# Gate and up products of a decoder's feed-forward as seven block products in place of eight

## The chip, the cores and the metric

The kernel runs on one core of one Trainium2 chip. The metric is the time of one execution on the device in microseconds (us); less is better. Five engines work from queues of their own and wait for each other by semaphores: TensorE (PE in the profile; its weight loads are PEld), VectorE (DVE), ScalarE (ACT), GpSimd (POOL) and SyncE (SP), which issues the DMAs.

## The reference, cut to what matters

Two layers, each with three groups of attention heads and then a feed-forward. Here only the feed-forward matters: 512 tokens, 1024 features, 2816 hidden features.

```python
for l in range(DEPTH):                      # DEPTH = 2
    x = x + concat(o_fox, o_diff, o_dsa) @ w_out[l]
    h = rms_norm(x, ffn_norm[l])
    gate, up = split(h @ w_gate_up[l], 2)   # 1024 x 2816 each
    x = x + (silu(gate) * up) @ w_down[l]
```

## The kernel before, in words

Everything is held transposed, features on the 128 partitions and the 512 tokens along a row; x is eight tiles of 128x512. Products are made at nearly float32 precision in three passes: each operand is split into a high part (ACT copies it to the rounded type fp32r) and a low part (what is left, a subtraction of two SBUF tiles, mostly on DVE), and `mm3` adds high x high, low x high and high x low into one PSUM tile (L172 to L174 of the profile).

The feed-forward of a layer (`feed_forward`):

- `split_input` makes yh and yl, the high and low parts of x times the norm's gain, eight tiles of each. `square_sum` adds the squares of x into `acc` (DVE, L213). `token_rms` sums `acc` over partitions on PE (ssq, L220) and takes the reciprocal root (the chain ends in r, L187). `norm_row` spreads r over partitions with four transposes on PE (rrow, L991) and copies it to R (L992). R is multiplied in after the products, so the products don't wait for it.
- The 2816 hidden features are 22 tiles of 128. For each tile f, `gate_up(f)` loads 2 x 512 KB of weights (u = 0 gate, u = 1 up; SP, L153), splits them (`weights`: ACT L159, DVE L162, four pieces of 128x512 each) and makes two products, each 8 x 3 matmuls of 128x512. `activate(f)` multiplies by R out of PSUM (DVE L964, L967), takes silu (ACT L965), multiplies gate and up (L968), and splits the result for the down product (gh by ACT L970, gl by DVE L972).
- `down` multiplies three groups of hidden tiles by w_down and adds to x (L984). The first group stands after tile 8, the second half after tile 15 and half after tile 21, the third at the end.

What sets the order: PE's queue is in program order (`manual_schedule`). The queues of ACT, DVE, POOL and SP come from the tile framework's scheduler, which takes priorities from the table AHEAD. Tile pools with a fixed number of buffers set what waits for what: a tile can be written again when its last reader is done. In the attention stages POOL makes low parts too (L162, `wl_in`, and L347, L550); in the feed-forward it has no work.

In the code `G` is POOL, `V` is DVE, `A` is ACT, `T` is PE and `SY` is SP.

Of the kernel before, what the change touches and what calls it, by code (L numbers as in the profile page):

```python
# [11 lines left out]
F32 = mybir.dt.float32  # L12
F32R = mybir.dt.float32r
# [4 lines left out]
P = 128  # L18
# [68 lines left out]
def trunk(ctx: ExitStack, tc: tile.TileContext, x_in, w_in, w_out, w_gu, w_dn, vecs, gfeat, rope, out):  # L87
# [9 lines left out]
    def mm_tile(name):  # L97
        return psum.tile([P, S], F32, tag="mm", name=name, bufs=3)
# [4 lines left out]
    def o_tile(name):  # L103
# [123 lines left out]
    def attention(l, ap):  # L227


        lam_init = 0.8 - 0.6 * math.exp(-0.3 * l)  # L230

        def xt_tile(name):
            return ap.tile([P, S], F32, tag="x", name=name, bufs=5)


        vec = const.tile([P, NV], F32, tag="vec", name=f"vec{l}")
        fb = vec[:, 0:FOX]
        fqn, fkn = vec[:, 8:72], vec[:, 72:136]
        dqn, dkn = vec[:, 136:168], vec[:, 168:200]
# [691 lines left out]
            pass  # L931

    def feed_forward(l, fp):
        y = split_input(l, 1, range(KT))
        acc = square_sum(fp, f"1{l}")
        R = fp.tile([P, S], F32, tag="R", name=f"R{l}")

        def gate_up(f, between=None):

            pgu = []  # L940
            for u in range(2):
                if u and between:
                    between()
                part = weights(w_gu[l, :, (2 * f + u) * KT * P:(2 * f + u + 1) * KT * P], KT * P, P, f"gu{l}_{f}_{u}")
# [17 lines left out]
        def activate(f, pgu):
            gs = fp.tile([P, S], F32, tag="gs", name=f"gs{l}_{f}", bufs=2)
            V.tensor_tensor(gs, pgu[0], R, op=ALU.mult)  # L964
            A.activation(gs, gs, AF.Silu)  # L965
            us = fp.tile([P, S], F32, tag="us", name=f"us{l}_{f}", bufs=2)
            V.tensor_tensor(us, pgu[1], R, op=ALU.mult)  # L967
            V.tensor_tensor(us, us, gs, op=ALU.mult)  # L968
            h = fp.tile([P, S], F32R, tag="gh", name=f"gh{l}_{f}", bufs=16)
# [28 lines left out]
        for f, ps in enumerate((pgu, nxt, after)):  # L998
            activate(f, ps)
        for f in range(3, NF):  # L1000
            activate(f, gate_up(f))

            if f == DOWN_GROUPS[0][1]:
                down(0, range(KT))
            if f == DOWN_GROUPS[1][1]:
                down(1, range(KT // 2))
        down(1, range(KT // 2, KT))
        down(2, range(KT))
# [75 lines left out]
```

## Time and profile before

| | |
|---|---|
| median of 3 runs | 1297.68 us (1296.26 to 1298.03) |
| the profiled execution, its own time | 1296.69 us |
| its span, first to last instruction | 1295.0 us |
| PE busy | 1270.0 us (98%) |
| DVE busy | 802.4 us (62%) |
| ACT busy | 653.9 us (50%) |
| POOL busy | 246.7 us (19%) |
| mean granted TensorE clock | 0.997 |

A span is the time between the first and the last instruction; the time of an execution is some 1.7 us longer. Busy shares are means over stages with different limits, and PE's is no measure of how close it is to its peak, since matmuls are pipelined: the spacing of their starts is what counts.

### The profile page before, as it was taken

Reading aid. Unit: us, or ns where it says so; the run is one execution under the profiler, and the core shown is the slowest. Engines: PE = TensorE matmul, PEld = TensorE weight load, DVE = VectorE, ACT = ScalarE, POOL = GpSimd, SP = SyncE. Lnnn points to the kernel's source line nnn. Section 1 sums busy time; section 2 is a strip of 40 time slices with the busy share of each in tenths; the row PEclk is TensorE's granted clock in tenths of the full one; section 3 lists DMA queues with packets and bytes.
Section 4 is the critical chain, followed back from the end, with each engine's and each line's share of the span. In section 5 each row is a group of like instructions: output and inputs, shape, how many; then the busy total and the mean of one; then the engine's idle time right before and its main releaser. Section 6 shows DMA issues by size and latency. Waiting matters only on the chain. (4 is left out here: it accounts for less than half of the span.)

```text
span 1295.0 us, 19339 instructions
## 1 busy us (share of the span) xinstructions
PE 1270.0 (98%) x7070; PEld 1081.2 (83%) x7070; DVE 802.4 (62%) x1829; ACT 653.9 (50%) x1510; POOL 246.7 (19%) x269
## 2 busy tenths in 40 slices
PE   9999999999999999999999899999999999999998
PEld 8988796788888888888899888968888888888887
DVE  5699996875544455444546999768755534444442
ACT  6678777864332233232456786768543323333321
POOL 2454465220000000000025545552100000000000
PEclk9999999999999999999999999999999999999999
DMA  5321121123333333332322212211333333333332
GB/s 183 90 76 51 56 86 34 57 70 102 105 94 93 96 96 93 110 94 87 103 79 82 75 50 63 66 45 52 96 98 98 97 92 92 97 100 102 92 95 99
DMA packets 34623, 111.55 MB, mean 86 GB/s; under 512 B 3952, under 2 KB 4448, under 8 KB 34528
## 3 DMA queue, kind: packets, MB, share of 16 engines
q1 hardware_dynamic: 34528, 110.31, 28.8%
q8 instruction: 56, 0.92, 0.3%
q14 instruction: 39, 0.32, 0.1%
HBM read 108.14 MB, written 2.15 MB: 85 GB/s over the span
## 5 line engine op out<-in xcount | busy, mean ns | idle before, releaser
L172 PE MATMUL gu<-yh,wh_gu 128*128 128x512 f32 x688 | 268.1, 390 | 0.0
L174 PE MATMUL gu<-yl,wh_gu 128*128 128x512 f32 x688 | 267.7, 389 | 0.0
L173 PE MATMUL gu<-yh,wl_gu 128*128 128x512 f32 x688 | 267.7, 389 | 0.0
L159 ACT ACTIVATE wh_gu<-raw_gu 128x512 fp32r<-128x512 f32 x176 | 111.0, 631 | 254.9 <-PE gu L174 205.6
L172 PE MATMUL pj<-wh_in,yh 128*128 128x256 f32 (+1 forms) x704 | 202.2, 287 | 0.9 <-ACT wh_in L159 0.7
L162 DVE TENSOR_TENSOR wl_gu<-raw_gu,wh_gu 128x512 fp32r<-128x512 f32 x176 | 121.8, 692 | 125.6 <-ACT wh_gu L159 123.1
L173 PE MATMUL pj<-wh_in,yl 128*128 128x256 f32 (+1 forms) x704 | 199.0, 283 | 0.4 <-DVE yl L201 0.4
L174 PE MATMUL pj<-wl_in,yh 128*128 128x256 f32 (+1 forms) x704 | 198.9, 283 | 0.2 <-DVE wl_in L162 0.2
L162 POOL TENSOR_TENSOR wl_in<-raw_in,wh_in 128x512 fp32r<-128x512 f32 x72 | 100.1, 1407 | 488.5 <-ACT wh_in L159 482.3
L172 PEld LDWEIGHTS gu<-yh,wh_gu 128*128 128x128 f32 x688 | 129.1, 188 | 26.8
L174 PEld LDWEIGHTS gu<-yl,wh_gu 128*128 128x128 f32 x688 | 129.1, 188 | 26.8
L173 PEld LDWEIGHTS gu<-yh,wl_gu 128*128 128x128 f32 x688 | 129.1, 188 | 26.8
L172 PE MATMUL dn<-gh,wh_dn 128*128 128x512 f32 x352 | 138.7, 394 | 0.0
L174 PE MATMUL dn<-gl,wh_dn 128*128 128x512 f32 x352 | 138.0, 392 | 0.0
L159 ACT ACTIVATE wh_dn<-raw_dn 128x512 fp32r<-128x512 f32 x96 | 57.3, 597 | 159.6 <-PE dn L174 111.5
L172 PEld LDWEIGHTS pj<-wh_in,yh 128*128 128x128 f32 x704 | 134.5, 191 | 3.0 <-issue 1.2
L173 PE MATMUL dn<-gh,wl_dn 128*128 128x512 f32 x352 | 136.6, 388 | 0.0
L173 PEld LDWEIGHTS pj<-wh_in,yl 128*128 128x128 f32 x704 | 134.9, 192 | 1.3 <-DVE yl L201 0.6
L174 PEld LDWEIGHTS pj<-wl_in,yh 128*128 128x128 f32 x704 | 134.8, 192 | 0.4 <-DVE wl_in L162 0.4
L162 DVE TENSOR_TENSOR wl_dn<-raw_dn,wh_dn 128x512 fp32r<-128x512 f32 x96 | 62.2, 648 | 68.7 <-ACT wh_dn L159 67.7
L174 PEld LDWEIGHTS dn<-gl,wh_dn 128*128 128x128 f32 x352 | 66.1, 188 | 15.5
L173 PEld LDWEIGHTS dn<-gh,wl_dn 128*128 128x128 f32 x352 | 66.1, 188 | 14.8
(323 smaller groups left out, 2167.9 us busy)
## 6 DMA issues: line engine op xcount, KB each, us to landing
raw_gu<-in_w_gu SPq DMA_DIRECT2D x88, 512.0 KB
raw_in<-in_w_in SPq DMA_DIRECT2D x39, 512.0 KB
raw_dn<-in_w_dn SPq DMA_DIRECT2D x32, 448.0 KB
raw_dn<-in_w_dn SPq DMA_DIRECT2D x16, 512.0 KB
cr<-rtd_c SPq DMA_DIRECT2D x12, 256.0 KB
raw_o_fox<-in_w_out SPq DMA_DIRECT2D x8, 384.0 KB
x<-in_x_in SPq DMA_DIRECT2D x8, 256.0 KB
raw_o_diff<-in_w_out SPq DMA_DIRECT2D x4, 512.0 KB
```

What stands on the lines that cost most here:

```text
L159: A.activation(h[:, :w], raw[:, o:o + w], AF.Copy)
L162: eng.tensor_tensor(lo[:, :w], raw[:, o:o + w], f32(h[:, :w]), op=ALU.subtract)
L172: T.matmul(ps, ah, bh, start=first, stop=False, skip_group_check=True)
L173: T.matmul(ps, al, bh, start=False, stop=False, skip_group_check=True)
L174: T.matmul(ps, ah, bl, start=False, stop=last, skip_group_check=True)
```

## The change

From the fourth tile on (`DIRECT = 3`) the gate and up products of a tile are made by `seven(f)` in place of `gate_up` and `activate`. The weights of a tile are a matrix of two row blocks (gate, up) by two column blocks (features 0 to 511 and 512 to 1023): a11, a12, a21, a22, each 128x512 in SBUF. The input is cut into four blocks too: two halves of the features by two halves of the tokens. Seven products of one weight block (or sum of blocks) with one input block (or sum) give all four blocks of the result, in Winograd's form of Strassen's scheme. Each product is 4 x 3 matmuls of 128x256.

- The four input sums of each of the four pairs of feature tiles are made once per layer by POOL (`input_sums`, 16 operations of 128x256) and split by ACT and DVE (8 operations each).
- The four weight sums of each tile are made by POOL (128x512 each), and the seven weight operands are split by ACT and DVE: seven operations of 128x512 each where there were four.
- After each product DVE (once ACT) combines halves: six DVE operations of 128x256 with one operand in PSUM, one of 128x256 in SBUF, and POOL multiplies the up half by R (128x512).
- `norm_row` stands ahead of the third tile, not in the middle of it.
- The hidden tiles of the down product are grouped (0, 7), (7, 14), (14, 22), each group's product in one piece; the tiles gh and gl have 8 buffers in place of 16, and some constants moved into the attention's pool, so that all fits in SBUF.

```diff
-DOWN_GROUPS = [(0, 8), (8, 15), (15, 22)]
+DOWN_GROUPS = [(0, 7), (7, 14), (14, 22)]
...
+        def input_sums(kt):
+            xg = []
+            for m in (kt, kt + KT // 2):
+                t = fp.tile([P, S], F32, tag="ws", name=f"xg{l}_{m}", bufs=5)
+                A.activation(t, x[m], AF.Copy, scale=gf[:, (2 * l + 1) * KT + m:(2 * l + 1) * KT + m + 1])
+                xg.append(t)
...
+            G.tensor_tensor(t1, b12, b11, op=ALU.subtract)
+            G.tensor_tensor(t3, b22, b12, op=ALU.subtract)
+            G.tensor_tensor(t2, b22, t1, op=ALU.subtract)
+            G.tensor_tensor(t4, b21, t2, op=ALU.subtract)
...
+        def seven(f):
...
+            a11, a12, a21, a22 = (r[:, o:o + half] for r in raws for o in (0, half))
+            sums = [fp.tile([P, half], F32, tag="ws", name=f"ws{l}_{f}_{i}", bufs=5) for i in range(4)]
+            with ahead("fh"):
+                G.tensor_tensor(sums[0], a21, a22, op=ALU.add)
+                G.tensor_tensor(sums[1], sums[0], a11, op=ALU.subtract)
+                G.tensor_tensor(sums[2], a11, a21, op=ALU.subtract)
+                G.tensor_tensor(sums[3], a12, sums[1], op=ALU.subtract)
...
+            def product(ps, w, k, first, last):
+                for kt in range(KT // 2):
+                    cs = slice(kt * P, (kt + 1) * P)
+                    mm3(ps, w[0][:, cs], w[1][:, cs], *Y[kt][k], first and kt == 0, last and kt == KT // 2 - 1)
...
+            product(a, whole(a11, "a"), "11", True, True)
+            with ahead("post"):
+                A.activation(u2, a, AF.Copy)
+            product(b, split_sum(sums[1], f"{l}_{f}_1", V), "T2", True, True)
+            with ahead("post"):
+                V.tensor_tensor(u2, b, u2, op=ALU.add)
+            product(d, split_sum(sums[2], f"{l}_{f}_2", V), "T3", True, True)
+            with ahead("post"):
+                V.tensor_tensor(us[:, H:], d, u2, op=ALU.add)
+            product(c, split_sum(sums[0], f"{l}_{f}_0", V), "T1", True, True)
+            with ahead("post"):
+                V.tensor_tensor(us[:, H:], c, us[:, H:], op=ALU.add)
+            product(a, whole(a12, "b"), "21", False, True)
+            with ahead("post"):
+                V.tensor_tensor(gs[:, :H], a, R[:, :H], op=ALU.mult)
+            product(d, whole(a22, "d"), "T4", False, True)
+            with ahead("post"):
+                V.tensor_tensor(us[:, :H], d, u2, op=ALU.add)
+            G.tensor_tensor(us, us, R, op=ALU.mult)
+            product(c, split_sum(sums[3], f"{l}_{f}_3", V), "22", False, True)
+            with ahead("post"):
+                V.tensor_tensor(gs[:, H:], c, u2, op=ALU.add)
+            V.tensor_tensor(gs[:, H:], gs[:, H:], R[:, H:], op=ALU.mult)
+            A.activation(gs, gs, AF.Silu)
+            V.tensor_tensor(us, us, gs, op=ALU.mult)
+            inner(f, us)
...
-        after = gate_up(2, norm_row)
...
+        for kt in range(KT // 2):
+            input_sums(kt)
+        norm_row()
...
+        for f in range(DIRECT, NF):
+            seven(f)
+
+            for g in range(len(DOWN_GROUPS) - 1):
+                if f == DOWN_GROUPS[g][1]:
+                    down(g, range(KT))
+        down(len(DOWN_GROUPS) - 1, range(KT))
```

(The last lines of `seven` are as in `activate`: `inner` splits us into gh and gl. `whole` and `split_sum` are one ACT copy and one DVE subtraction of 128x512 each.)

DVE's queue while PE makes tile 11 of layer 0 (wl_gu and wsl are low parts of weights, ws the sums that POOL makes). Before, a stretch in which one tile's work stands:

```order
L972 TENSOR_TENSOR gl0_10_5367<-us0_10_5362,gh0_10_5365 128x512
L162 TENSOR_TENSOR wl_gu0_12_0_512_5457<-raw_gu0_12_0_5449,wh_gu0_12_0_512_5455 128x512
L964 TENSOR_TENSOR gs0_11_5439<-gu0_11_0_5379,R0_4178 128x512
L162 TENSOR_TENSOR wl_gu0_12_1_0_5488<-raw_gu0_12_1_5484,wh_gu0_12_1_0_5486 128x512
L162 TENSOR_TENSOR wl_gu0_12_1_512_5492<-raw_gu0_12_1_5484,wh_gu0_12_1_512_5490 128x512
L967 TENSOR_TENSOR us0_11_5442<-gu0_11_1_5414,R0_4178 128x512
L162 TENSOR_TENSOR wl_gu0_13_0_0_5533<-raw_gu0_13_0_5529,wh_gu0_13_0_0_5531 128x512
L968 TENSOR_TENSOR us0_11_5442<-us0_11_5442,gs0_11_5439 128x512
```

And now, twelve of a tile's sixteen rows; the other four are u2 of product b ahead of them, and, behind them, the low part of the weights' sum 1 of tile 13, the product of us and gs, and the low part of a22 of tile 13:

```order
L975 TENSOR_TENSOR gl0_10_5943<-us0_10_5816,gh0_10_5941 128x512
L1023 TENSOR_TENSOR wsl_0_12_2_6146<-ws0_12_2_6097,wsh_0_12_2_6144 128x512
L1067 TENSOR_TENSOR us0_11_5962<-gu0_11_d_5960,u20_11_5963 128x256
L1023 TENSOR_TENSOR wsl_0_12_0_6163<-ws0_12_0_6095,wsh_0_12_0_6161 128x512
L1070 TENSOR_TENSOR us0_11_5962<-gu0_11_c_5958,us0_11_5962 128x256
L1023 TENSOR_TENSOR wsl_0_12_3_6215<-ws0_12_3_6098,wsh_0_12_3_6213 128x512
L1073 TENSOR_TENSOR gs0_11_5961<-gu0_11_a_5957,R0_4178 128x256
L1047 TENSOR_TENSOR wl_gu0_13_a_6258<-raw_gu0_13_0_6237,wh_gu0_13_a_6256 128x512
L1076 TENSOR_TENSOR us0_11_5962<-gu0_11_d_5960,u20_11_5963 128x256
L1047 TENSOR_TENSOR wl_gu0_13_b_6326<-raw_gu0_13_0_6237,wh_gu0_13_b_6324 128x512
L1080 TENSOR_TENSOR gs0_11_5961<-gu0_11_c_5958,u20_11_5963 128x256
L1081 TENSOR_TENSOR gs0_11_5961<-gs0_11_5961,R0_4178 128x256
```

Eight operations a tile became sixteen, and between a combination out of PSUM (gu) and the next there now stands one low part of the next tile's or the next but one's weights.

POOL's queue over the same tile, empty before (ws 0 to 3 are the four sums):

```order
L1077 TENSOR_TENSOR us0_11_5962<-us0_11_5962,R0_4178 128x512
L1037 TENSOR_TENSOR ws0_14_1_6388<-ws0_14_0_6387,raw_gu0_14_0_6383 128x512
L1038 TENSOR_TENSOR ws0_14_2_6389<-raw_gu0_14_0_6383,raw_gu0_14_1_6385 128x512
L1039 TENSOR_TENSOR ws0_14_3_6390<-raw_gu0_14_0_6383,ws0_14_1_6388 128x512
L1036 TENSOR_TENSOR ws0_15_0_6797<-raw_gu0_15_1_6795 128x512
L1077 TENSOR_TENSOR us0_12_6108<-us0_12_6108,R0_4178 128x512
```

Five operations a tile, and the product of us and R, which DVE's product of us and gs waits for, stands behind the sums of tiles further on.

PE's queue where the transposes for R stand in layer 0. Before:

```order
L174 MATMUL gu0_2_0_4345<-yl10_7_4153,wh_gu0_2_0_512_4341 128x512
L991 MATMUL rrow0_4370<-ident_80,r10_4291 128x128 x4
L172 MATMUL gu0_2_1_4386<-yh10_0_4123,wh_gu0_2_1_0_4378 128x512
L173 MATMUL gu0_2_1_4386<-yh10_0_4123,wl_gu0_2_1_0_4380 128x512
L174 MATMUL gu0_2_1_4386<-yl10_0_4125,wh_gu0_2_1_0_4378 128x512
```

And now:

```order
L168 MATMUL gu0_1_1_4310<-yl10_7_4153,wh_gu0_1_1_512_4306 128x512
L1102 MATMUL rrow0_4407<-ident_80,r10_4291 128x128 x4
L166 MATMUL gu0_2_0_4443<-yh10_0_4123,wh_gu0_2_0_0_4435 128x512
L167 MATMUL gu0_2_0_4443<-yh10_0_4123,wl_gu0_2_0_0_4437 128x512
L168 MATMUL gu0_2_0_4443<-yl10_0_4125,wh_gu0_2_0_0_4435 128x512
```

They moved half a tile (24 matmuls) up, and all of the third tile's matmuls now stand behind them.

## Rows read from the trace of the kernel before

**Rows 1.** The page's parts 1 and 2: busy time, POOL over 40 slices.

```profile
PE 1270.0 (98%) x7070; PEld 1081.2 (83%) x7070; DVE 802.4 (62%) x1829; ACT 653.9 (50%) x1510; POOL 246.7 (19%) x269
...
POOL 2454465220000000000025545552100000000000
```

**Rows 2.** Windows of layer 0: gate and up (f 0 to 8), then down.

```profile
core 0: us, PE busy (x) PEld busy (x) DVE busy (x) ACT busy (x) POOL busy (x), PEclk, DMA share, GB/s
288.00:387.20 99.20, 99.20 (x445) 82.19 (x444) 54.89 (x87) 38.63 (x63) 0.00 (x0) 1.00 0.33 97
387.30:431.20 43.90, 43.90 (x193) 36.01 (x192) 17.77 (x26) 10.76 (x17) 0.00 (x0) 1.00 0.33 96
```

**Rows 3.** Timeline of DVE over one tile (start us, us, what).

```profile
559.63 0.69 DVE L967 TENSOR_TENSOR us<-gu,R 128x512 f32<-128x512 f32 x1 [1.30 <-PE gu L174]
560.35 0.69 DVE L162 TENSOR_TENSOR wl_gu<-raw_gu,wh_gu 128x512 fp32r<-128x512 f32 x1
560.96 0.69 DVE L968 TENSOR_TENSOR us<-us,gs 128x512 f32<-128x512 f32 x1
...
570.52 0.69 DVE L967 TENSOR_TENSOR us<-gu,R 128x512 f32<-128x512 f32 x1 [1.30 <-PE gu L174]
```

**Rows 4.** Timeline of PE: first and last of 36 projection matmuls, back to back.

```profile
19.20 0.30 PE L172 MATMUL pj<-wh_in,yh 128*128 128x256 f32 x1
...
23.40 0.28 PE L174 MATMUL pj<-wl_in,yh 128*128 128x256 f32 x1
```

**Rows 5.** Groups by form: count, busy us, mean ns, idle before.

```profile
L162 DVE TENSOR_TENSOR wl_gu<-raw_gu,wh_gu 128x512 fp32r<-128x512 f32 x176 | 121.8, 692 | 125.6 <-ACT wh_gu L159 123.1
...
L471 DVE TENSOR_TENSOR pt_s<-t_s,pt_s 128x256 fp32r<-128x256 f32 x48 | 19.6, 418 | 6.9 <-ACT pt_s L467 6.7
...
L159 ACT ACTIVATE wh_gu<-raw_gu 128x512 fp32r<-128x512 f32 x176 | 111.0, 631 | 254.9 <-PE gu L174 205.6 <-PE dn L174 38.3 <-PE wo_dsa L174 4.2
```

**Rows 6.** Timeline of DVE: two operations of 128x256 back to back.

```profile
263.30 0.76 DVE L471 TENSOR_TENSOR pt_s<-t_s,pt_s 128x256 fp32r<-128x256 f32 x2 [0.45 <-ACT pt_s L467]
```

**Rows 7.** Timeline of POOL, three stretches of the attention of layer 0.

```profile
78.89 1.44 POOL L550 TENSOR_TENSOR hq_d<-raw_d,hq_d 128x256 fp32r<-128x256 f32 x2 [3.58 <-ACT hq_d L548]
...
121.17 1.86 POOL L162 TENSOR_TENSOR wl_in<-raw_in,wh_in 128x512 fp32r<-128x512 f32 x1 [3.43 <-ACT wh_in L159]
122.98 2.28 POOL L347 TENSOR_TENSOR hq_f<-raw_f,hq_f 128x512 fp32r<-128x512 f32 x1
...
157.44 1.30 POOL L347 TENSOR_TENSOR hq_f<-raw_f,hq_f 128x512 fp32r<-128x512 f32 x1 [2.17 <-ACT hq_f L346]
```

**Rows 8.** Timeline of DVE beside the last two stretches of rows 7.

```profile
121.80 2.31 DVE L333 TENSOR_TENSOR raw_f<-raw_f,rn_f 128x1024 f32<-128x1024 f32 x1
...
124.43 1.39 DVE L397 TENSOR_TENSOR raw_f<-raw_f,gfox 128x512 f32<-128x512 f32 x1
...
158.60 0.40 DVE L471 TENSOR_TENSOR pt_f<-t_f,pt_f 128x256 fp32r<-128x256 f32 x1
```

**Rows 9.** Timelines of PE and DVE at the feed-forward's start, layer 0.

```profile
288.00 0.39 PE L950 MATMUL gu<-yh,wh_gu 128*128 128x512 f32 x1
...
304.35 0.95 PE L220 MATMUL ssq<-ones,acc 128*128 128x2 f32 x8
316.13 0.60 PE L991 MATMUL rrow<-ident,r 128*128 128x128 f32 x4
...
288.51 0.68 DVE L812 TENSOR_TENSOR x<-wo_dsa,x 128x512 f32<-128x512 f32 x1
...
306.61 0.16 DVE L187 TENSOR_TENSOR r<-rst_x,rsy_x 128x4 f32<-128x4 f32 x1
```

**Rows 10.** Windows in layer 1's attention, columns as in rows 2.

```profile
786.00:790.30 4.30, 2.60 (x15) 1.67 (x14) 4.30 (x17) 1.80 (x8) 1.83 (x5) 1.00 0.41 124
790.40:793.80 3.40, 3.40 (x18) 3.30 (x16) 3.40 (x11) 2.62 (x8) 1.48 (x3) 0.50 0.02 5
```

More of the change, by code (lines that the diff above doesn't have):

```diff
@@ L141, in trunk, with weights @@
     ss32 = rp[:, 160:192].rearrange("p (b e) -> p b e", b=NB)
-    vals = [const.tile([P, NB, 2, 2, 64], F32R, name=f"vals{i}") for i in range(3)]
-    svals = const.tile([P, NB, 2, 64], F32R, name="svals")
     dram = ctx.enter_context(tc.tile_pool(name="dram", bufs=1, space=bass.MemoryType.DRAM))
-    def weights(src, n, step, name, eng=V, load=None):
+    def weights(src, n, step, name, eng=V, load=None, hi="wh"):
         raw = wp.tile([P, 1024], F32, tag="raw", name=f"raw_{name}", bufs=2)
@@ L158, in weights @@
             h = wp.tile([P, 512], F32R, tag="wh", name=f"wh_{name}_{o}")
-            A.activation(h[:, :w], raw[:, o:o + w], AF.Copy)
+            with ahead(hi):
+                A.activation(h[:, :w], raw[:, o:o + w], AF.Copy)
             lo = wp.tile([P, 512], F32R, tag="wl", name=f"wl_{name}_{o}")
@@ L203, in split_input, with square_sum @@
         return parts
-    def square_sum(pool, name):
-        acc = pool.tile([P, S], F32, tag="acc", name=f"acc{name}", bufs=3)
+    def square_sum(pool, name, tags=(("acc", 3), ("x", 5))):
+        acc = pool.tile([P, S], F32, tag=tags[0][0], name=f"acc{name}", bufs=tags[0][1])
         with ahead("ssq"):
@@ L230, in attention @@
         lam_init = 0.8 - 0.6 * math.exp(-0.3 * l)
+        vals = [ap.tile([P, NB, 2, 2, 64], F32R, tag=f"vals{i}", name=f"vals{l}_{i}") for i in range(3)]
+        svals = ap.tile([P, NB, 2, 64], F32R, tag="svals", name=f"svals{l}")
+        causal = ap.tile([P, S], F32, tag="causal", name=f"causal{l}")
+        cdiag = causal[:, S - P:]
+        G.memset(causal, 0.0)
+        G.affine_select(out=cdiag, in_=cdiag, compare_op=ALU.is_ge, fill=BIG, base=0,
+                        pattern=[[-1, P]], channel_multiplier=1)
         def xt_tile(name):
             return ap.tile([P, S], F32, tag="x", name=name, bufs=5)
-        vec = const.tile([P, NV], F32, tag="vec", name=f"vec{l}")
+        vec = ap.tile([P, NV], F32, tag="vec", name=f"vec{l}")
         fb = vec[:, 0:FOX]
@@ L934, in feed_forward @@
         y = split_input(l, 1, range(KT))
-        acc = square_sum(fp, f"1{l}")
+        acc = square_sum(fp, f"1{l}", (("gh", GH), ("gl", GH)))
         R = fp.tile([P, S], F32, tag="R", name=f"R{l}")
+        half = KT // 2 * P
+        H = S // 2
         def gate_up(f, between=None):
@@ L943, in gate_up @@
                     between()
[L944 removed]
+                part = weights(w_gu[l, :, (2 * f + u) * KT * P:(2 * f + u + 1) * KT * P], KT * P, P, f"gu{l}_{f}_{u}", hi="fh")
                 ps = (st_tile if u else mm_tile)(f"gu{l}_{f}_{u}")
@@ L960, in feed_forward, with inner @@
         gt = {}
[L962 to L969, printed above, removed]
+        def inner(f, us):
+            h = fp.tile([P, S], F32R, tag="gh", name=f"gh{l}_{f}", bufs=GH)
@@ new lines, in split_sum, with whole @@
+        def split_sum(src, name, eng):
+            h = fp.tile([P, half], F32R, tag="wsh", name=f"wsh_{name}", bufs=5)
+            with ahead("fh"):
+                A.activation(h, src, AF.Copy)
+            lo = fp.tile([P, half], F32R, tag="wsl", name=f"wsl_{name}", bufs=5)
+            with ahead("wl"):
+                eng.tensor_tensor(lo, src, f32(h), op=ALU.subtract)
+            return h, lo
+        def seven(f):
+            raws, parts = [], {}
+            for u in range(2):
+                raw = (fp if u else wp).tile([P, 1024], F32, tag="raw", name=f"raw_gu{l}_{f}_{u}", bufs=2)
+                SY.dma_start(raw, w_gu[l, :, (2 * f + u) * KT * P:(2 * f + u + 1) * KT * P])
+                raws.append(raw)
+            a11, a12, a21, a22 = (r[:, o:o + half] for r in raws for o in (0, half))
+            sums = [fp.tile([P, half], F32, tag="ws", name=f"ws{l}_{f}_{i}", bufs=5) for i in range(4)]
+            with ahead("fh"):
+                G.tensor_tensor(sums[0], a21, a22, op=ALU.add)
+                G.tensor_tensor(sums[1], sums[0], a11, op=ALU.subtract)
+                G.tensor_tensor(sums[2], a11, a21, op=ALU.subtract)
+                G.tensor_tensor(sums[3], a12, sums[1], op=ALU.subtract)
+            def whole(src, k):
+                h = wp.tile([P, 512], F32R, tag="wh", name=f"wh_gu{l}_{f}_{k}")
+                with ahead("fh"):
+                    A.activation(h, src, AF.Copy)
+                lo = wp.tile([P, 512], F32R, tag="wl", name=f"wl_gu{l}_{f}_{k}")
+                with ahead("wl"):
+                    V.tensor_tensor(lo, src, f32(h), op=ALU.subtract)
+                return h, lo
+            def product(ps, w, k, first, last):
+                for kt in range(KT // 2):
+                    cs = slice(kt * P, (kt + 1) * P)
+                    mm3(ps, w[0][:, cs], w[1][:, cs], *Y[kt][k], first and kt == 0, last and kt == KT // 2 - 1)
+            a, c = (mm_tile(f"gu{l}_{f}_{k}")[:, :H] for k in "ac")
+            b, d = (st_tile(f"gu{l}_{f}_{k}")[:, :H] for k in "bd")
+            gs, us = pair(f)
+            u2 = fp.tile([P, H], F32, tag="u2", name=f"u2{l}_{f}", bufs=2)
+            product(a, whole(a11, "a"), "11", True, True)
[14 more added lines that the diff above has]
+            product(d, whole(a22, "d"), "T4", False, True)
+            with ahead("post"):
+                V.tensor_tensor(us[:, :H], d, u2, op=ALU.add)
+            G.tensor_tensor(us, us, R, op=ALU.mult)
+            product(c, split_sum(sums[3], f"{l}_{f}_3", V), "22", False, True)
+            with ahead("post"):
+                V.tensor_tensor(gs[:, H:], c, u2, op=ALU.add)
+            V.tensor_tensor(gs[:, H:], gs[:, H:], R[:, H:], op=ALU.mult)
+            A.activation(gs, gs, AF.Silu)
+            V.tensor_tensor(us, us, gs, op=ALU.mult)
+            inner(f, us)
@@ L996, in feed_forward @@
         nxt = gate_up(1, lambda: rstd.extend(token_rms(acc, f"1{l}")))
-        after = gate_up(2, norm_row)
-        for f, ps in enumerate((pgu, nxt, after)):
-            activate(f, ps)
-        for f in range(3, NF):
-            activate(f, gate_up(f))
[L1003 to L1008, printed above, removed]
+        for kt in range(KT // 2):
+            input_sums(kt)
+        norm_row()
+        activate(0, pgu)
+        activate(1, nxt)
+        for f in range(2, DIRECT):
+            activate(f, gate_up(f))
+        for f in range(DIRECT, NF):
[4 more added lines that the diff above has]
+        down(len(DOWN_GROUPS) - 1, range(KT))
     with tc.manual_schedule(engines={mybir.EngineType.PE}):
```

32 lines of the change are left out of this document (24 added, 8 removed).

## The prediction

> **What bounds the kernel now.** I read the busy times first, then windows of the feed-forward, then single tiles. PE is busy 98% of the span, DVE 62%, and POOL's slices are zero in both feed-forwards [rows 1]. In the gate and up window PE is busy all of 99.2 us at the full granted clock (1.00), DVE 54.9, ACT 38.6, POOL nothing, and the DMAs take a third of their time; in the down window DVE works 17.8 of 43.9 us [rows 2]. So PE sets the pace there. A tile lasts from the first us to the next, 559.63 to 570.52: 10.89 us, and DVE's waits in it end with PE [rows 3]. It is 48 matmuls of 512 columns, 0.227 us apart.
>
> **PE alone.** The 36 projection matmuls of 256 columns, also with a new weight load each, start 4.20 us apart from first to last, 35 steps of 0.120 us [rows 4]. Half the columns thus cost 53% of the spacing, not 50%. A tile becomes 7 x 4 x 3 = 84 such matmuls: 84 x 0.120 = 10.08 us, 0.81 less. With 19 tiles a layer and two layers, 38 x 0.81 = 31 us is the most that the change can give; seven for eight would suggest 52. The down matmuls are as many as before, in other groups: nothing.
>
> The Trainium skill (TensorE: Matmul & The Clock Gate, section "Wait — 56ns, not 53.3ns?") gives a warm matmul its columns over 2.4 GHz and 2.5 ns more; by that a tile would save 1.2 us and the whole 45 us. The rows' 227 and 120 ns are above it at both widths, and decide.
>
> **DVE and POOL per tile.** DVE's queue has 16 operations a tile. Nine are 128x512 with both operands in SBUF (seven low parts, us times gs, gl), one is 128x256 in SBUF, six are 128x256 with one operand in PSUM. Unhindered, a 512 one follows the other after 0.61 us (560.35 to 560.96, [rows 3]); two of 256 take 0.76 together, the last of them 0.42 [rows 5, 6], so 0.34 apart. 9 x 0.61 + 7 x 0.34 = 7.9 us, below 10.08. ACT's ten operations, at most 0.63 each [rows 5], make 6.3 us: covered. POOL has five of 128x512, 1.30 each when nothing stands in the way [rows 7]: 6.5 us. The loads are the same bytes, in a third of the DMAs' time [rows 2]: covered. Each engine alone would fit into PE's 10.08 us.
>
> But POOL and DVE don't run side by side when DVE reads two SBUF tiles. POOL's operation of 121.17 ends at 123.03; DVE's raw_f, started at 121.80, ends at 124.11, 1.08 after it; POOL's next ends 1.15 after that (125.26, 2.28 us for a 1.30 us operation); DVE's next ends at 125.82, 0.56 later (1.39 for 0.69) [rows 7, 8]. They take turns. An operation that reads PSUM does not: pt_f at 158.60 takes its 0.40 beside POOL's 1.30 [rows 7, 8]. Ten of DVE's sixteen are of the kind that waits, and all five of POOL's.
>
> So each POOL operation that starts holds DVE at its next such operation. In the new order at most one PSUM operation (0.34) stands between, and POOL's sums are released just there, by the low part that frees the buffer ws. DVE stands 1.30 less 0.34, some 0.95 us, at each (0.8 to 1.2 by where it falls). 5 x 0.95 = 4.8, and 7.9 + 4.8 = **12.7 us** a tile, above PE's 10.08 and above the old 10.89. The turn-taking closes on itself: us times gs waits for POOL's us times R, and everything behind it in DVE's queue, next tile's low parts and combinations that free PSUM, waits with it. So PE can't run ahead by more than the one tile of weights that five buffers hold. The bounds of this term: no hold at all, 10.1 (PE); no overlap at all, 7.9 + 6.5 = 14.4. I take the middle since the order alternates PSUM and SBUF operations.
>
> The Trainium skill (SBUF — State Buffer, section "SBUF: two separate sides") says that whoever starts first has the shared ports for its whole instruction. By that the nine and a half DVE operations at 0.69 and POOL's 6.5 us make 13.1 us a tile on the ports alone; the rows show less, since POOL resumes before DVE's recorded end (1.15 for a 1.30 us operation).
>
> How many tiles: the downs cut a layer's 19 into runs of 5, 7 and 7. The first of a run finds its weights made while DVE had room in the down window [rows 2], and near the end POOL has no more sums to make, so I count two tiles of each run at PE's 10.08: (3 + 5 + 5) x 12.7 + 6 x 10.08 = 225.6 against 19 x 10.89 = 206.9. **+18.7 us a layer.**
>
> **The feed-forward's start.** Before, DVE adds the last x at 288.51, PE sums acc at 304.35, r ends at 306.8, and PE needs it at 316.13 [rows 9]: 9 us to spare. Now the transposes stand after the second tile, 288.0 + 2 x 10.89 = 309.8. Between the last x and r DVE's queue holds 26 operations of 128x512 (eight of them the new low parts of input sums) and a few small ones: 26 x 0.61 + 0.8 = 16.7 us. In the same time POOL makes its 16 sums of 128x256, 0.72 each [rows 7], and the first of tile 3. If each of the 16 holds DVE by 0.55 (0.72 less the overlap at its ends seen above) and three of tile 3's by 1, that is 12 more: r at 288.5 + 28.7 = 317. PE waits some 7 us, and nothing of the third tile can pass. Bounds: 0 if nothing holds, 12 if each held its full length. **+7 us a layer.**
>
> At the end of the last run, silu, product and split of tile 21 (some 3.5 us by the same rows) hide behind 21 matmuls of the other seven hidden tiles (4.8 us). Moved constants: nothing on the path.
>
> **Sum.** 2 x (18.7 + 7) = +51 on the profiled execution's 1296.7 (span 1295.0), that is 1348; the median of the runs is 1.0 above it: **1349 us**, 4% slower.
>
> **Rivals.**
> - *POOL's work fits into gaps* (faster). Each engine is under 10.08 us, and holds that fall where DVE waits for PE cost nothing. Then PE bounds: 1297.7 - 31 = 1267. Against it: 7.9 of 10.08 leaves 2.2 us of gaps for five holds. Chance 0.14.
> - *Break-even.* Holds of half the size give 11.0 a tile and 2 to 3 us at the start: within some 5 us of 1298. Chance 0.05 (0.03 within 0.2%, which is about what a measurement of this kernel can tell from no change; 0.01 to either side).
> - *Turns without overlap*: 14.4 us a tile, 12 at the start. 2 x (13 x 14.4 + 6 x 10.08 - 206.9 + 12) = +106: 1403. It decides where the wait for us times R falls while DVE has nothing to do. Chance 0.09.
> - *The clock falls.* After PE had stood 1.7 of 4.3 us, a stretch of 3.4 us had the granted clock at 0.50, its lower level of 1.2 GHz [rows 10]. Standing 7 us at the transposes could bring one in each layer (+1.7 each, inside my range). If it came in each of 26 slowed tiles, 44 more: 1393. Against it: the waits in a tile are cut into pieces of some 0.4 us between products. Chance 0.06.
> - That fewer matmuls aren't issued can be left out: the order shows 84 of 128x256 a tile.
>
> **The numbers.** My forecast 0.66; of it and the others, slower 0.66 + 0.09 + 0.06 + 0.01 = 0.82, same 0.03, faster 0.14 + 0.01 = 0.15. The range reaches from 1308 (12.0 us a tile at DVE holds of 0.8, no wait at the start: 2 x (13 x 12.0 + 60.5 - 206.9) = +19, less some) to 1403, the worst of the cases; left out are the faster and the even one, 0.14 + 0.05 = 0.19.
>
> **What would show it.** Right: tiles of some 12.7 us with DVE nearly full and operations of two SBUF tiles of 1 to 2 us mean, those out of PSUM still 0.42; POOL's over 1.3; PE's idle time ended by ACT's and DVE's weight parts; a wait of about 7 us before rrow. Wrong: tiles of 10.1 us with PE full and DVE's waits ended by PE, or low parts still at 0.69 beside a busy POOL.

## The result, and the profile after

The changed kernel takes 1354.56 us (median of four runs, 1353.95 to 1356.63) against 1297.66: a ratio of 1.0443 with a 95% interval of 1.0425 to 1.0461. The forecast was 1349 in a range of 1308 to 1403. The profiled execution took 1354.94 us, its span is 1353.2, 58.2 above that of before. The page's part 1, and POOL over the 40 slices of part 2:

```profile
PE 1264.2 (93%) x8438; PEld 1136.9 (84%) x8438; DVE 1080.4 (80%) x2149; ACT 736.0 (54%) x1694; POOL 557.0 (41%) x493
...
POOL 2554554345514640652024545633554065326510
```

Against [rows 1], PE has lost five points of its share, and DVE gained 18 with POOL's 19 to 41. From the starts of PE's matmuls, both layers together, the 58.2 us are (to rounding):

| | before | after | |
|---|---|---|---|
| feed-forward's first matmul to tile 3 | 68.1 | 91.8 | +23.7 |
| tiles 3 to 21, 38 of them | 413.6 | 451.3 | +37.7 |
| down products | 241.3 | 241.3 | 0 |
| attention, which the change leaves alone | | | -3.1 |

The prediction had +37.4 for the tiles and +14 for the start.

**One tile.** DVE from one `gs` out of gu_a to the next, 479.42 to 492.32, 12.90 us where [rows 3] had 10.89 (start us, us, what, and in brackets the idle time before):

```profile
479.42 0.41 DVE L1073 TENSOR_TENSOR gs<-gu_a,R 128x256 f32<-128x256 f32 x1
479.75 1.67 DVE L1047 TENSOR_TENSOR wl_gu_a<-raw_gu,wh_gu_a 128x512 fp32r<-128x512 f32 x1
481.34 0.41 DVE L1076 TENSOR_TENSOR us<-gu_d,u 128x256 f32<-128x256 f32 x1
481.68 0.68 DVE L1047 TENSOR_TENSOR wl_gu_b<-raw_gu,wh_gu_b 128x512 fp32r<-128x512 f32 x1
482.28 0.41 DVE L1080 TENSOR_TENSOR gs<-gu_c,u 128x256 f32<-128x256 f32 x1
482.72 1.07 DVE L1081 TENSOR_TENSOR gs<-gs,R 128x256 f32<-128x256 f32 x1
483.72 0.68 DVE L1023 TENSOR_TENSOR wsl<-ws,wsh 128x512 fp32r<-128x512 f32 x1
484.56 1.81 DVE L1083 TENSOR_TENSOR us<-us,gs 128x512 f32<-128x512 f32 x1 [0.17 <-ACT gs L1082]
...
488.43 0.41 DVE L1067 TENSOR_TENSOR us<-gu_d,u 128x256 f32<-128x256 f32 x1
488.77 1.65 DVE L1023 TENSOR_TENSOR wsl<-ws,wsh 128x512 fp32r<-128x512 f32 x1
490.34 0.41 DVE L1070 TENSOR_TENSOR us<-gu_c,us 128x256 f32<-128x256 f32 x1
490.68 1.72 DVE L1023 TENSOR_TENSOR wsl<-ws,wsh 128x512 fp32r<-128x512 f32 x1
492.32 0.41 DVE L1073 TENSOR_TENSOR gs<-gu_a,R 128x256 f32<-128x256 f32 x1
```

POOL in the same stretch:

```profile
479.57 1.30 POOL L1036 TENSOR_TENSOR ws<-raw_gu 128x512 f32<-128x512 f32 x1 [0.63 <-DVE wsl L1023]
481.83 1.68 POOL L1077 TENSOR_TENSOR us<-us,R 128x512 f32<-128x512 f32 x1 [0.96 <-DVE us L1076]
484.53 1.29 POOL L1037 TENSOR_TENSOR ws<-ws,raw_gu 128x512 f32<-128x512 f32 x1 [1.02 <-issue]
488.59 1.29 POOL L1038 TENSOR_TENSOR ws<-raw_gu,raw_gu 128x512 f32<-128x512 f32 x1 [2.77 <-DVE wsl L1023]
490.56 1.28 POOL L1039 TENSOR_TENSOR ws<-raw_gu,ws 128x512 f32<-128x512 f32 x1 [0.69 <-DVE wsl L1023]
```

Read the two side by side. POOL has five operations, and five of DVE's are long, each beside one of POOL's. From each of these five to DVE's next start it is 1.59, 1.00, 1.74, 1.57 and 1.64 us where 0.61 (0.34 for L1081) is the unhindered spacing: 0.98 + 0.66 + 1.13 + 0.96 + 1.03 = 4.8 us of holds. The operations out of PSUM that run beside POOL (L1073, L1080, L1067, L1070) stay at 0.41; L1080 lies wholly inside POOL's 1.68 us. An operation of two SBUF tiles while POOL is idle (483.72) takes 0.68. So does that of 481.68, which started before POOL's: there POOL is the one held, 1.68 us for 1.29.

**Who PE waits for.** PE's longest waits over the whole span (us in total, times, longest):

```profile
PE gu_d L166 <- DVE us L1067: 45.4, 26, 4.3
PE rrow L1102 <- DVE r L181: 14.4, 2, 7.2
```

In the tile above, PE's wait is this one:

```profile
488.90 0.39 PE L166 MATMUL gu_d<-Yh_t,wh_gu_d 128*128 128x256 f32 x1 [2.18 <-DVE us L1067]
```

The sixth product adds to the PSUM tile gu_d, and can't begin until DVE has read the third product out of it (L1067). That is DVE's operation at 488.43. PE had gone on from the third product to the next at 483.70, so its result had been there for over 4 us; L1067 stands in DVE's queue behind held operations. The 38 tile periods of the trace have a mean of 11.88 us: 9.95 for the first of the later runs, 15 to 16 for their second, 10.4 to 14.1 for those behind it, 9.95 again for the last.

**The groups by form** (count, busy us, mean ns, idle before), to be read against [rows 5]:

```profile
L1023 DVE TENSOR_TENSOR wsl<-ws,wsh 128x512 fp32r<-128x512 f32 x152 | 167.9, 1111 | 2.1 <-ACT wsh L1020 1.8
L1047 DVE TENSOR_TENSOR wl_gu_a<-raw_gu,wh_gu_a 128x512 fp32r<-128x512 f32 x38 | 51.5, 1354 | 0.8 <-ACT wh_gu_a L1044 0.8
...
L1067 DVE TENSOR_TENSOR us<-gu_d,u 128x256 f32<-128x256 f32 x38 | 15.6, 412 | 0.0
```

**The start.** DVE and then PE in layer 0, to be read against [rows 9]:

```profile
312.80 0.15 DVE L216 TENSOR_SCALAR ms<-ssq 128x4 f32<-128x4 f32 x1
312.87 1.74 DVE L156 TENSOR_TENSOR wl_gu<-raw_gu,wh_gu 128x512 fp32r<-128x512 f32 x1
314.52 1.23 DVE L178 TENSOR_TENSOR rst_x<-rsy_x 128x4 f32<-128x4 f32 x1
315.79 1.20 DVE L179 TENSOR_TENSOR rst_x<-rst_x,ms 128x4 f32<-128x4 f32 x1
317.02 1.20 DVE L180 TENSOR_SCALAR rst_x<-rst_x 128x4 f32<-128x4 f32 x1
318.25 0.16 DVE L181 TENSOR_TENSOR r<-rst_x,rsy_x 128x4 f32<-128x4 f32 x1
...
318.47 1.12 PE L1102 MATMUL rrow<-ident,r 128*128 128x128 f32 x4 [7.21 <-DVE r L181]
```

POOL beside the three operations of 128x4:

```profile
314.01 1.72 POOL L1038 TENSOR_TENSOR ws<-raw_gu,raw_gu 128x512 f32<-128x512 f32 x1
315.69 1.27 POOL L1039 TENSOR_TENSOR ws<-raw_gu,ws 128x512 f32<-128x512 f32 x1
316.92 1.27 POOL L1036 TENSOR_TENSOR ws<-raw_gu 128x512 f32<-128x512 f32 x1
```

L178, L179 and L180 end as these three do, one by one, where the same operations took 0.15 to 0.17 us before. r ends at 318.41, and PE has stood 7.21 us for it.

### The profile page after: what moved, and what is told of

Read it like the earlier page. It is cut to its first block, busy times and chain, and to the rows that moved or that the text cites. A ratio compares the mean times of both kernels' runs of the same rounds, so it can differ in the third digit from the quotient of the medians.

```text
span 1353.2 us, 23112 instructions
## 1 busy us (share of the span) xinstructions
PE 1264.2 (93%) x8438; PEld 1136.9 (84%) x8438; DVE 1080.4 (80%) x2149; ACT 736.0 (54%) x1694; POOL 557.0 (41%) x493
## 5 line engine op out<-in xcount | busy, mean ns | idle before, releaser
L1023 DVE TENSOR_TENSOR wsl<-ws,wsh 128x512 fp32r<-128x512 f32 x152 | 167.9, 1111 | 2.1 <-ACT wsh L1020 1.8
L1020 ACT ACTIVATE wsh<-ws 128x512 fp32r<-128x512 f32 x152 | 89.0, 622 | 65.6 <-PE gu_c L168 35.7
L156 DVE TENSOR_TENSOR wl_dn<-raw_dn,wh_dn 128x512 fp32r<-128x512 f32 x96 | 70.5, 734 | 58.8 <-ACT wh_dn L153 58.3
L1037 POOL TENSOR_TENSOR ws<-ws,raw_gu 128x512 f32<-128x512 f32 x38 | 52.6, 1385 | 135.5 <-DMA raw_gu<-in_w_gu 118.1
L1077 POOL TENSOR_TENSOR us<-us,R 128x512 f32<-128x512 f32 x38 | 59.2, 1558 | 113.4 <-DVE us L1076 113.4
L166 PE MATMUL gu_d<-Yh_t,wh_gu_d 128*128 128x256 f32 x152 | 48.8, 321 | 45.4 <-DVE us L1067 45.4
L1038 POOL TENSOR_TENSOR ws<-raw_gu,raw_gu 128x512 f32<-128x512 f32 x38 | 55.3, 1454 | 58.1 <-DVE wsl L1023 58.1
L1082 ACT ACTIVATE gs<-gs 128x512 f32<-128x512 f32 x38 | 24.0, 632 | 100.5 <-DVE gs L1081 100.5
L166 PEld LDWEIGHTS dn<-gh,wh_dn 128*128 128x128 f32 x352 | 66.1, 188 | 14.4
L168 PEld LDWEIGHTS dn<-gl,wh_dn 128*128 128x128 f32 x352 | 66.3, 188 | 13.1
```

The source lines that it names most:

```text
L1020: A.activation(h, src, AF.Copy)
L1023: eng.tensor_tensor(lo, src, f32(h), op=ALU.subtract)
L1037: G.tensor_tensor(sums[1], sums[0], a11, op=ALU.subtract)
L1038: G.tensor_tensor(sums[2], a11, a21, op=ALU.subtract)
L1077: G.tensor_tensor(us, us, R, op=ALU.mult)
```

## The experiments

The theory T is that of the prediction: POOL and DVE take turns wherever DVE reads two SBUF tiles, so POOL's help costs DVE more than it saves. Rivals: DVE's queue is too long and POOL relieves it; PE's wait for gu_d is the bound by itself; the sums are slow because results pass from engine to engine; the place of `norm_row` costs the start.

**x_alldve: POOL's five operations a tile on DVE.**

```diff
-                G.tensor_tensor(sums[0], a21, a22, op=ALU.add)
+                V.tensor_tensor(sums[0], a21, a22, op=ALU.add)
...
-            G.tensor_tensor(us, us, R, op=ALU.mult)
+            V.tensor_tensor(us, us, R, op=ALU.mult)
```

(and the other three sums alike)

> The changed kernel with the four weight sums and us times R of each tile on DVE; POOL keeps only the input sums. Turn-taking theory (DVE is held at each POOL operation that it meets): DVE has 21 operations a tile, 7.9 + 5 x 0.61 = 10.95 us, and no holds, so the inner tiles go from 12.9 to about 10.9 us and the first and last of a run stay at 9.95; 2 x 13 x 2.0 = 52 us less, and some 2 us per layer at the start because tile 3's sums no longer hold DVE: 1295 to 1305 us. Rival (what counts is the work in DVE's queue, and POOL takes work off it): 3.05 us more in each of 26 tiles, 1354.6 + 79 = 1434 us, with DVE's operations at their old durations. Rival (PE's wait for the PSUM tile d is the bound by itself): within 5 us of 1354.6.

Measured: 1270.86 us, ratio to before 0.9806 (0.9782 to 0.983). T's sign holds and both rivals fall: DVE has five operations more in each tile, and the kernel is 84 us faster. The size was missed by 24 us: I expected inner tiles of 10.9, and of 38 tiles 34 take 9.95 to 10.03. DVE over seven tiles (columns as in [rows 2]):

```profile
413.50:483.30 69.80, 69.80 (x590) 69.78 (x589) 67.98 (x133) 36.62 (x64) 0.00 (x0) 1.00 0.32 101
```

It is 133 operations, 19 a tile and not 21: 16 of the run's weight sums and low parts were made in the down window ahead of it (375.1 to 413.5), and six operations for the down products fall into it. 68.0 of 69.8 us: DVE just keeps up, and PE never stands. In the groups by form the low parts of the sums are back at one length:

```profile
L1023 DVE TENSOR_TENSOR wsl<-ws,wsh 128x512 fp32r<-128x512 f32 x152 | 102.6, 681 | 0.7
```

**x_ghost: x_alldve, and POOL has work that nobody needs.**

```diff
                 V.tensor_tensor(sums[3], a12, sums[1], op=ALU.subtract)
+                G.tensor_tensor(idle, a21, a22, op=ALU.subtract)
+                G.tensor_tensor(idle, a22, a11, op=ALU.subtract)
+                G.tensor_tensor(idle, a11, a21, op=ALU.subtract)
+                G.tensor_tensor(idle, a12, a22, op=ALU.subtract)
```

> The kernel of x_alldve, and POOL makes four more subtractions of 128x512 a tile out of the raw weights into a tile of its own that nothing reads. Turn-taking theory: though nothing waits for POOL's results, each of them holds DVE by some 0.95 us where it meets DVE: inner tiles of about 10.95 + 4 x 0.95 = 14.7 us, less where POOL's four come in a row and the last two of a row find DVE at a PSUM operation; 45 to 95 us above x_alldve. Rival (the sums were slow because of the chain from POOL's result to the weight splits, not because of a shared way into SBUF): within 5 us of x_alldve, DVE's low parts at 0.69.

Measured: 1411.05 us, 140 above x_alldve. No engine reads what POOL writes, and the time is worse than that of the change. DVE and POOL, while POOL makes three of the four in a row and after it:

```profile
431.02 1.78 DVE L1024 TENSOR_TENSOR wsl<-ws,wsh 128x512 fp32r<-128x512 f32 x1
432.72 1.78 DVE L1052 TENSOR_TENSOR wl_gu_a<-raw_gu,wh_gu_a 128x512 fp32r<-128x512 f32 x1
434.43 1.77 DVE L1024 TENSOR_TENSOR wsl<-ws,wsh 128x512 fp32r<-128x512 f32 x1
436.12 0.68 DVE L1037 TENSOR_TENSOR ws<-raw_gu 128x512 f32<-128x512 f32 x1
436.72 0.68 DVE L1052 TENSOR_TENSOR wl_gu_b<-raw_gu,wh_gu_b 128x512 fp32r<-128x512 f32 x1
```

```profile
430.47 1.78 POOL L1042 TENSOR_TENSOR idle<-raw_gu,raw_gu 128x512 f32<-128x512 f32 x1 [0.52 <-DMA raw_gu<-in_w_gu]
432.33 1.63 POOL L1043 TENSOR_TENSOR idle<-raw_gu,raw_gu 128x512 f32<-128x512 f32 x1
434.04 1.61 POOL L1044 TENSOR_TENSOR idle<-raw_gu,raw_gu 128x512 f32<-128x512 f32 x1
```

This is the plainest view of the turns: one operation of DVE's and one of POOL's go every 1.70 us. Once POOL has ended (435.65), DVE's next start (436.12) and the one behind it are 0.60 apart. So the chain from POOL to the weight splits is not needed for the loss; the shared time is enough. My 45 to 95 us were exceeded, though most inner tiles of the later runs take 11.4 to 14.2 us and not 14.7. I had counted 13 tiles a layer: the mean is 13.0 over all 19 (55 us a layer above x_alldve), and tile 3, the first of them, takes 22 us where it took 12. The first tile behind each inner down product also starts 6.2 us later, when DVE's addition of the last down product to x (L1100), which frees a PSUM tile, comes late in its queue. POOL reads the raw weights too and could delay the next load, but DVE's waits for those loads sum to 7.4 us in the whole run, against 5.7 in x_alldve, and ACT and PE have none, so late loads explain next to none of it.

**x_room: the kernel before, with four such subtractions a tile.**

```diff
+        if name.startswith("gu"):
+            G.tensor_tensor(idle[-1], raw[:, :512], raw[:, 512:], op=ALU.subtract)
+            G.tensor_tensor(idle[-1], raw[:, 512:], raw[:, :512], op=ALU.subtract)
```

> The kernel before the change, and POOL makes four subtractions of 128x512 per hidden tile out of the raw weights into a tile of its own that nothing reads. Turn-taking theory: DVE's low parts stretch here too (those of the weights to a mean over 1.0 us), but DVE has room: its tile is 5.5 us of work plus at most 4 x 0.95 of holds, 9.3 us, below PE's 10.89; the time stays within 0.4% of before, up to 6 us more for the two starts. Rival (every hold costs its length in the time): 2 x 22 x 4 x 0.95 = 167 us slower.

Measured: 1299.51 us, ratio 1.002 (1.0008 to 1.0031), as T has it. DVE's low parts of the weights, 692 ns in [rows 5], are held here too:

```profile
L164 DVE TENSOR_TENSOR wl_gu<-raw_gu,wh_gu 128x512 fp32r<-128x512 f32 x176 | 182.3, 1037 | 97.6 <-ACT wh_gu L161 96.8
```

The low parts alone are 60 us longer, and the time is 2.4 us longer. Tiles 3 to 21 take the same 413.6 us as before; the starts of the two layers, in which DVE's operations stand back to back for some 10 us, are 2.9 and 2.5 us longer. So holds cost time only where DVE has no room left.

**x_two: two of the four sums back on POOL.**

```diff
-                V.tensor_tensor(sums[0], a21, a22, op=ALU.add)
+                G.tensor_tensor(sums[0], a21, a22, op=ALU.add)
...
-                V.tensor_tensor(sums[2], a11, a21, op=ALU.subtract)
+                G.tensor_tensor(sums[2], a11, a21, op=ALU.subtract)
```

> The kernel of x_alldve with two of the four weight sums (the first and the third, which read raw weights alone) back on POOL. Turn-taking theory: DVE saves 2 x 0.61 = 1.2 us a tile and gets two holds of 0.95 = 1.9 us, 0.7 us more in a tile whose DVE was full at 9.95 to 10: inner tiles of 10.6 to 11.4 us, 13 a layer, and some us more at the start: 1288 to 1310 us. Rival (less work for DVE is faster): 1268 to 1271 us, as x_alldve, which PE bounds.

Measured: 1318.78 us, 48 above x_alldve; the rival falls, and my range was 9 us short. Inner tiles are 11.05 and 11.43, as expected, but the first of each later run is 12.4 to 12.9 (I had taken the ends of a run at 9.95), and tile 3 begins 5.7 us later in each layer, most of it at rrow, where PE waits 5.2 us for r and not 1.7. DVE in one tile, the two held operations:

```profile
453.36 1.66 DVE L975 TENSOR_TENSOR gl<-us,gh 128x512 fp32r<-128x512 f32 x1
454.94 0.68 DVE L1023 TENSOR_TENSOR wsl<-ws,wsh 128x512 fp32r<-128x512 f32 x1
...
457.41 1.45 DVE L1047 TENSOR_TENSOR wl_gu_a<-raw_gu,wh_gu_a 128x512 fp32r<-128x512 f32 x1
```

The 19 operations unhindered are 7.9 + 3 x 0.61 = 9.7 us, the holds 0.97 + 0.77: 11.5, and 11.43 are there. The sum of the prediction works with two holds as with five.

**x_usr: us times R alone on DVE.** In the changed kernel DVE stands idle for POOL four times, in the second tile of each later run (us in total, times, longest):

```profile
DVE us L1083 <- POOL us L1077: 11.0, 4, 3.7
```

In the first of the four, us is there for POOL at 437.87, and POOL's queue has five sums ahead of it:

```profile
437.30 1.29 POOL L1036 TENSOR_TENSOR ws<-raw_gu 128x512 f32<-128x512 f32 x1 [8.65 <-DMA raw_gu<-in_w_gu]
...
443.40 1.29 POOL L1036 TENSOR_TENSOR ws<-raw_gu 128x512 f32<-128x512 f32 x1
444.66 1.28 POOL L1077 TENSOR_TENSOR us<-us,R 128x512 f32<-128x512 f32 x1
```

```diff
-            G.tensor_tensor(us, us, R, op=ALU.mult)
+            V.tensor_tensor(us, us, R, op=ALU.mult)
```

> The changed kernel with us times R alone on DVE; the four weight sums and the input sums stay on POOL. In the changed kernel's second tile of the later runs (16 us) DVE stands 3.69 us for us times R, which is ready for POOL at 437.9 and waits behind five sums in POOL's queue until 444.66. Holds as summed: DVE gets 0.61 more and one hold of 0.95 less a tile, so the inner tiles go from 12.9 to some 12.5 (26 of them, 9 us less); and if the in-order queue of POOL makes the second tile long, those four tiles fall from 15 to 16 to about 13, some 11 us more: 1330 to 1340 us. Rival (the second tile is long because DVE has split too few weights in the down window): the four tiles stay at 15 to 16 us, and the time is 1343 to 1347 us.

Measured: 1340.11 us, 14.5 less than the change where some 20 were expected, at the edge of the first case. The four tiles go from 16.1, 15.4, 16.1 and 15.0 us to 13.1, 13.1, 14.4 and 13.0, and the inner ones from 12.9 to 12.6. The rival (too few weights split in the down window) falls. So the changed kernel has a second, smaller loss beside the turns: an in-order queue in which an urgent operation stands behind work for a later tile.

**x_isum: the input sums on DVE.**

```diff
-            G.tensor_tensor(t1, b12, b11, op=ALU.subtract)
+            V.tensor_tensor(t1, b12, b11, op=ALU.subtract)
```

(and t3, t2, t4 alike)

> The changed kernel with the 16 input sums per layer on DVE, nothing else. Turn-taking theory: DVE has 16 x 0.34 = 5.4 us more to do before r, and 16 holds less, 0.55 each = 8.8 us: r some 3.4 us earlier, PE's wait ahead of rrow 3 to 4 us in place of 7.2; with the clock perhaps not falling behind it (2.3 us more per layer): 1343 to 1349 us. Rival (work in DVE's queue alone counts): 2 x 5.4 = 11 us slower, 1365 us.

Measured: 1347.62 us, 7 less than the change, and the rival falls again. Of the steps in between I was wrong: the wait ahead of rrow is gone (it starts at 309.76, not 318.47) and tile 3 begins 7 to 8 us earlier after the feed-forward's first matmul. But that tile then takes 15.3 and 15.6 us where it took 10.4 and 11.0, and PE stands 3.5 us ahead of it, not for weights but until DVE's L984 takes an old product out of PSUM. L984 needs R, and ACT copies R (L1103) only at 320.89, 10.5 us after the transposes, behind splits of sums in its queue; two held low parts of DVE's stand between that and L984. More than half of what r gained is given back one tile later.

**x_mid: `norm_row` back in the middle of tile 2.**

```diff
-        norm_row()
...
-        for f in range(2, DIRECT):
-            activate(f, gate_up(f))
+        after = gate_up(2, norm_row)
...
+        activate(2, after)
```

> The changed kernel with norm_row back in the middle of tile 2, as before the change. If PE's order is what costs the 7.2 us ahead of rrow, 24 matmuls (5.45 us) go ahead of it and each layer gains some 5.4 us, and the clock has less of a pause: 1340 to 1344 us. If the start is bound by DVE's queue as a whole (R late, the low parts of tile 2's and tile 3's weights behind it), the wait only moves: PE then stands for weights or for free PSUM tiles a few us later, and the time stays within 4 us of 1354.6.

Measured: 1354.58 us against 1354.56: in the time the second case, but not for its reason. The wait ahead of rrow falls from 7.2 to 1.8 us, and 5.3 and 3.9 us of waiting turn up ahead of tile 3, again for L984 (at 327.60 in layer 0). DVE stands idle 3.8 and 2.5 us shortly before it, so most of this wait is not its queue. L984 needs R, and the copy of R stands in ACT's queue behind the high part of a sum that POOL starts only at 322.97, when its weights have come:

```profile
324.26 0.63 ACT L1020 ACTIVATE wsh<-ws 128x512 fp32r<-128x512 f32 x1 [7.12 <-POOL ws L1037]
...
325.44 0.60 ACT L1103 ACTIVATE R<-rrow 128x512 f32<-128x512 f32 x1
```

The transposes had ended at 317.60; in the changed kernel the copy follows them at once (319.59, 319.62). So moving `norm_row` back gains nothing with this order of ACT's queue. What it would gain with the copy of R further ahead is not shown, and that DVE's queue as a whole binds the start isn't either.

**x_best2 and x_best: what beats both kernels.** x_best2 is x_alldve with the edits of x_isum and x_mid and `DIRECT = 4`.

> A version that may beat both: x_alldve, with the input sums on DVE too, norm_row back in the middle of tile 2, and the seven products from the fifth tile on (DIRECT = 4), so that POOL has no work in the feed-forward and DVE has one tile more for the input sums. What x_alldve still lost by its rows: 1.7 us ahead of rrow, some 1.6 us in tile 3 and 0.8 in a later one, per layer; given back: 0.94 for the tile that is made the old way. 2 x (1.7 + 1.6 + 0.8 - 0.9) = 6 us less than x_alldve: 1262 to 1268 us. Rival (the input sums' 5.4 us on DVE only move the wait): 1270 to 1276 us.

Measured: 1262.57 us, ratio to before 0.9739 (0.9723 to 0.9755), 8.3 less than x_alldve. POOL has no work in the feed-forward; 34 of 36 tiles take 9.95 to 9.99 us. PE's longest wait for a product's PSUM tile is now

```profile
PE gu_d L166 <- DVE us L1067: 1.6, 2, 0.8
```

x_best also moves R from the up half of each hidden tile to the down product's result:

```diff
-            G.tensor_tensor(us, us, R, op=ALU.mult)
...
-                V.tensor_tensor(x[m], ps, x[m], op=ALU.add)
+                V.tensor_tensor(dr, ps, R, op=ALU.mult)
+                V.tensor_tensor(x[m], dr, x[m], op=ALU.add)
```

> x_best2, with R multiplied into the down products (one more DVE operation of 128x512 for each of the 24, the same result by the linearity of the product) in place of the up half of each hidden tile: DVE has 20 operations, 10.3 us, in place of 21 a tile. If DVE's queue is what still holds PE now and then, 1 to 3 us less than x_best2; if PE bounds all tiles, the same within 1 us, plus 0.6 us for the operation added at the end: 1260 to 1268 us.

Measured: 1263.69 us, 1.1 more than x_best2, and the ranges of the two touch. All 36 tiles are at 9.95 us, which is 2.2 us less in the tiles than x_best2, and the whole is no shorter: in the profiled executions the end is 0.7 us longer (the operation added) and the attention, whose code is the same, 1.4 us. PE bounds nearly all tiles of both versions, so one operation less on DVE shows no gain in these times.

## Why the prediction was right

- **The bound and the mechanism** were right: DVE and POOL take turns over operations of two SBUF tiles. x_ghost shows the loss with no data passing, x_alldve its end when POOL is idle in the tiles, x_room that it needs a full DVE. One row was weaker than I read it: pt_f of [rows 8] shares only 0.14 us with POOL's operation (158.60 to 158.74). That operations out of PSUM aren't held is shown by L1080 of the changed kernel.
- **The tile.** 7.9 + 5 x 0.95 = 12.7 was forecast, 12.90 and holds of 4.8 are there. In three cases the hold is where I put it, at the low part behind one PSUM operation; us times R meets gs times R, and the remaining sum (L1037) meets us times gs. The rule of the Trainium skill in the prediction (SBUF — State Buffer, section "SBUF: two separate sides") gave 13.1 us; the measured 12.90 lies between it and my sum. The two streams of x_ghost take 1.70 a pair where 1.25 and 0.61 alone would make 1.86, so each turn gives back some 0.16 us of its recorded length.
- **Which tiles.** Two of each run at 10.08 and the rest at 12.7 made 225.6 us a layer; 225.8 and 225.5 are there. But the shape is another: the second tile of the later runs takes 15 to 16 us, because us times R waits in POOL's queue behind five sums (x_usr), where I had named that wait and put no price on it; the tiles near the end of a run take 10.4 to 11.4 and make up for it. That the layer's total fits to 0.1% is luck.
- **PE alone** was mis-sized by a little: 9.95 us and not 10.08, 84 matmuls 0.1185 apart. What the change could give was 36 us, not 31, and x_alldve and x_best2 collect most of it (26 and 35 us less than before).
- **The start** is the term that was off: +7 us a layer forecast, +12.5 and +11.2 measured. The wait itself agrees (7 forecast, 7.2 measured), but by luck: two misses cancel. r came 31.8 us after the last x and not 28.7: the small operations of r's reciprocal root were taken at 0.8 us together, and L178, L179 and L180 were held 1.2 us each by POOL's sums for tile 3. And PE came to the transposes 25.2 us after its first matmul, not 21.8: ssq (0.9 us) was left out, and waits at the first product's inputs and at ssq made the stretch up to ssq 18.5 us where it was 16.4. These 2.2 us are one part that the sum lacked. The other is the clock. After the wait its granted share was at 0.50, which I had priced (1.7 us) and left out of the sum: matmuls of 512 columns start 0.427 apart from 319.81 to 324.08, and tile 2 takes 13.4 us in layer 0 and 12.2 in layer 1 where it took 10.9. x_mid and x_isum take the wait at rrow away, and another comes up ahead of tile 3, with R's copy 6.5 to 10.5 us behind the transposes in ACT's queue. In x_best2, where POOL makes no sums and tile 3 is made the old way, the starts are 34.75 us each, 0.7 above those of before. How much of the +12 lies in holds and how much in such orders of the queues stays open.
- **What ends PE's waits** was named wrongly. I wrote ACT's and DVE's weight parts; 45.4 us end with L1067, which empties gu_d. The backlog is the same, but it reaches PE by a combination that frees PSUM.
- **The clock rival** came true in part: the mean granted clock is 0.981 where it was 0.997. My reason against it was wrong: the waits in a tile aren't cut into pieces of 0.4 us, most of them stand in one piece of some 2.2 us ahead of the sixth product. Yet in the tiles compared here it cost nothing, because DVE sets their pace. Two tiles of layer 0 at the full clock take 25.82 us (first start to first start), two of layer 1 with a stretch at the lower one 25.73. In windows of 25.8 us, columns as in [rows 2]:

```profile
466.50:492.30 25.80, 21.00 (x170) 20.19 (x169) 25.37 (x33) 10.81 (x20) 13.95 (x10) 1.00 0.27 80
1136.70:1162.50 25.80, 22.34 (x171) 21.73 (x170) 25.40 (x34) 10.80 (x20) 13.64 (x10) 0.93 0.28 80
```

- The attention is 1.9 and 1.1 us shorter in this profile. The change leaves its operations alone, and profiles of the other versions differ by as much there; it stays unexplained.
- **The range.** Its lower end, 1308, is not what its sum gives: 1297.7 + 19 is 1317, and nothing stands behind the "less some". The measured time is far from it.

The gain that PE alone would have is real, and it went into the turns: where the tiles could be 36 us shorter they are 38 longer, the starts are 24 longer, and 84 us come back when the tiles' arithmetic is taken from POOL and given to DVE.

## What to carry to other kernels

In this kernel, moving an operation of 128x512 with two SBUF operands from DVE to POOL saves DVE 0.61 us and costs it about 0.95. That costs next to nothing while DVE has room (x_room), and it lost time where DVE was the next bound (the change and x_two, against x_alldve). Count both engines' operations that read two SBUF tiles as one queue. To put POOL's work beside stretches in which DVE reads PSUM would follow from the rows; it was not tried. Where an in-order engine is behind, the wait that the profile shows is only the first place where the delay meets PE: taking that wait away let another come up behind it (x_isum, x_mid), and taking POOL's work out of the tiles removed most of both (x_alldve, whose two starts are 15 us shorter together). Look at each engine's queue anew after such a move: in x_mid it was ACT's.

## What was not expected of the hardware

A hold lasts as long as POOL's operation does, however short DVE's is: three operations of 128x4 took 1.20 to 1.23 us each in a row while POOL worked on 128x512, and one of them (L180) reads a single SBUF tile. And the dearest work of all was work that nobody needed: four subtractions a tile whose results nothing reads cost 140 us in x_ghost and 2.4 in x_room.
